# A decoder layer's head: loads in order of need, one square per bank summed from SBUF, x's squares spread, six slot numbers moved

## The chip, the cores and the metric

The kernel is one program on one core of a Trainium2 chip. The metric is the time of one execution on the device in microseconds (us). Before the change it is 2418.71 us, the median of three runs (2417.26 to 2421.04).

The core has five engines that run their own instruction streams: PE (TensorE, the matrix multiplies), DVE (VectorE), ACT (ScalarE), POOL (GpSimd) and SP (SyncE, which here issues most of the transfers). They meet at semaphores only. Data lie in DRAM, in SBUF (128 partitions) and, for what PE accumulates, in the eight banks of PSUM.

## What is computed

One hybrid decoder layer on 512 tokens of width 2048, in fp32:

```
h = rms_norm(x, g_mix);  z = h @ w_in      # columns: attn q,k,v | ret q,k,v | ret gate
a = moba_attention(rope(rms_norm(q)), rope(rms_norm(k)), v)     # 8 heads of 128
r = silu(gate) * rms_norm(retention(rope(q), rope(k), v)) * g_ret   # 8 heads of 128
x = x + concat(a, r) @ w_o
h2 = rms_norm(x, g_ffn);  x = x + (silu(h2 @ w_gate) * (h2 @ w_up)) @ w_down
x = x + (p @ w_ple_proj) * sigmoid(rms_norm(x, g_ple) @ w_ple_gate + b)
```

Two norms matter here. The row norm of x (its 16 blocks of 128 x 512 are squared and summed) is not applied to h; its factor `rstd[0]` is applied to what is made of h. Query and key are normed for each head of 128 columns; the squares for that norm are those that the change rewrites.

## The kernel before

**Products.** Every fp32 operand is split into a high part and the remainder: `split` lets ACT write the high part (`wh` of a weight, `h`'s high half) and DVE subtract it (`wl`, the low half). A product is three matmuls: high by high, high by low, low by high (`mm3`, L73 to L76). For a weight unit of 128 x 1024 (`raw`, 512 KB) that is one ACT and one DVE instruction; `wh` and `wl` have three buffers each.

**Stages.** (1) `Plain`: the query and key columns of head pair 0, eight weight units of 24 matmuls, which accumulate into four banks (Y0, Y1, Z0, Z1). Beside it the 16 chunks of x transposed are loaded, scaled by ACT (`h_chunk`, L445) and split into `h`. (2) Three `Group`s of `w_vg` (values, values, gates). A Group forms a 1024-column block by seven products, in the order 1, 5, 6, 3, 7, 2, 4, of four units and twelve matmuls each; between products DVE adds weight quarters (`plus` on `raw`, L82). Products 5, 6, 3 and 7 need sums of chunks of x too: `first_factors(k)`, k from 0 to 7, loads chunks 2k and 2k+1 once more, into two buffers each (tags `e1`, `e5`), and makes the factors `s` from them (DVE L79, ACT, DVE L55). (3) The "mix": four attention pairs and four retention pairs. While a pair's projection runs (32 slots of six matmuls, some 1.36 us each), the score and weight products of the pair before it are put between the slots by hand: `heads` gives slot numbers to `at_slot`. (4) `w_ow`, the gate/up, down and per-layer-embedding products, all as Groups.

**The head's callback.** `run` goes through the steps of stages 1 and 2, from i = -3; at step i it multiplies step i, splits step i+2 and adds for step i+3, and calls `beside(i)` first: chunks of x for `h` and Plain's weights (i from -2 to 5), `first_factors` (i from 5 to 12), first weights of the Groups (i from 3), and two of the sixteen `xn` loads with their squares at each step from 17 to 24.

**What sets the order.** A scheduler orders the instructions of each engine at build time, by its own model. Only what goes through `keep_in_program_order` stays as written: all of PE's work in the mix does; in the head before nothing does. Buffers tie steps together: `x`, `xn`, `zeros` and the copies `z0` share four buffers of tag `o`, and a load into one waits until its last reader is done. SP issues its loads in order: one that waits holds all behind it.

**Pair norms.** `evac` in `qk_attn` takes one bank: DVE multiplies by the two rotary tables (`z`, and `m` in two halves), ACT squares each head's 128 columns with a running sum (`squares`, L437: four ACTIVATEs and four reads of the accumulator), DVE adds `z` and `m`, and a `tensor_scalar` and a power on POOL make the norm factor `rs`, by which ACT scales the key columns (L670). The projection of the next pair writes the same four banks, so each bank is free once its last reader here is done. Pair 0's `z` comes from DRAM, stored at Plain's end; its squares were taken from the banks there (`ms0`).

Of the kernel before, what the change touches and what calls it, by code (L numbers as in the profile page):

```python
# [10 lines left out]
F32 = mybir.dt.float32  # L11
# [22 lines left out]
def layer_kernel(ctx, tc, x, xT, pT, g_mix, wqk, w_vg, qk_norm, g_ret, w_ow, g_ffn,  # L34
# [46 lines left out]
    def plus(o, a, b):  # L81
        nc.vector.tensor_tensor(o, a, b, op=ALU.add)  # L82
# [122 lines left out]
    class Group:  # L205
# [8 lines left out]
        def load(self, q, u):  # L214
            t = rawq.tile([P, 2, T], F32, name="raw", tag={"11": "l1", "12": "bd"}.get(q, "c"))
            nc.sync.dma_start(t, self.src(int(q[0]) - 1, int(q[1]) - 1, self.units[u]))
            self.raw[q, u] = t
# [178 lines left out]
    class Plain:  # L396
# [5 lines left out]
        def load(self, u):  # L402
            self.raw[u] = rawq.tile([P, 2, T], F32, name="raw", tag="l1" if u < 4 else "c")
            nc.sync.dma_start(self.raw[u], wqk[0, u])

# [3 lines left out]
        def extract(self, p, u):  # L409
            self.w[u] = [wq.tile([P, 2, T], F32R, name=n, tag=n) for n in ("wh", "wl")]  # L410
            split(*self.w[u], self.raw[u])

# [12 lines left out]
        def evac(self):  # L425
            for b in range(NB):
                t = ev_tile("o", 4, name="z0")
                nc.scalar.activation(t, self.acc[b], AF.Copy)
                nc.sync.dma_start(zd[b], t)
                squares(ms0[b], ev_tile("v", name="sq"), self.acc[b])  # L430

    zd = [dram.tile([P, T], F32, name=f"z_{b}") for b in range(NB)]
    ms0 = [stat.tile([P, 4], F32, name="ms0", bufs=NB) for _ in range(NB)]

    def squares(ms, junk, of):
        for j in range(4):
            nc.scalar.activation(junk[:, j * HD:(j + 1) * HD], of[:, j * HD:(j + 1) * HD],  # L437
                                 AF.Square, accum_out=ms[:, j:j + 1])

    first = Plain()  # L440

    def h_chunk(k, tag="o", bufs=4):
        t = ev_tile(tag, bufs, name="x")
        nc.sync.dma_start(t, xT[k * P:(k + 1) * P, :])
        nc.scalar.activation(t, t, AF.Copy, scale=gm[:, k:k + 1])  # L445
        return t
# [37 lines left out]
    groups[0].next, groups[1].next = groups[1:]  # L484
    nc.sync.dma_start(ident, ident_c)
    nc.sync.dma_start(gf, g_ffn)
    nc.sync.dma_start(gp, g_ple)
    nc.sync.dma_start(gr, g_ret)

    def beside(i):  # L490

        if -2 <= i < NC // 2 - 2:
            for k in (2 * i + 4, 2 * i + 5):
                t = h_chunk(k)
                split(h[:, k, 0, :], h[:, k, 1, :], t)
            first.load(i + 2)
        if 5 <= i < 5 + NC // 2:
            first_factors(i - 5)
        for at, q in ((3, "11"), (7, "12"), (11, "22")):
            if at <= i < at + 4:  # L500
                groups[0].load(q, i - at)
        if 17 <= i < 25:
            for u in range(2):
                b, s = divmod(2 * (i - 17) + u, NS)
                t = ev_tile("o", 4, name="xn")
                nc.sync.dma_start(t, x[b * P:(b + 1) * P, s * T:(s + 1) * T])
                nc.scalar.activation(t, t, AF.Square, accum_out=ssq[0][:, b, s:s + 1])
        elif i == 25:
            rstd_of(ssq[0], rstd[0])
# [135 lines left out]
    def qk_attn(i):  # L645

        made, norms = [], []

        def evac(b, acc, ms=None):
            z = rp_tile("z", (P, 2, 2, HD))  # L650
            m = rm_tile("m", (P, 2, 2, 2, HD // 2))
            a4 = acc.rearrange("p (s h d) -> p s h d", s=2, h=2)
            a5 = acc.rearrange("p (s h u e) -> p s h u e", s=2, h=2, u=2)
# [3 lines left out]
            for u in range(2):  # L657
                nc.vector.tensor_tensor(m[:, :, :, u], a5[:, :, :, 1 - u],
                                        sn[:, :, b, None, u * half:(u + 1) * half].to_broadcast([P, 2, 2, half]),
                                        op=ALU.mult)  # L660
            if ms is None:
                ms = stat.tile([P, 4], F32, name="ms")
                squares(ms, rm_tile("sq"), acc)
            plus(z, z, m.rearrange("p s h u e -> p s h (u e)"))
            nc.vector.tensor_scalar(ms, ms, 1.0 / HD, eps1[:, b:b + 1], op0=ALU.mult, op1=ALU.add)
            rs = stat.tile([P, 4], F32, name="rs", tag="rsqk", bufs=2 * NB)
            power(rs, ms, 4)
            z3 = z.rearrange("p s h d -> p (s h) d")
            for j in (2, 3):
# [4 lines left out]
        if i == 0:  # L674
            for b in range(NB):
                evac(b, z0[:, b].rearrange("p c e -> p (c e)").bitcast(F32), ms0[b])
        else:
            for b, acc in enumerate(projection(True)):
                evac(b, acc)
        return made, norms  # L680
# [160 lines left out]
    def heads(i, made):  # L841
# [5 lines left out]

        at_slot(17 if i <= NPAIR else 8, lambda: v.append(v_of(i)))
        if i < NPAIR:
# [7 lines left out]
            if i == 0:  # L857
                plan = [(n + 3, fn) for n, fn in plan]
        else:
            for j, (at, steps_s, steps_n, last) in enumerate(((8, (11, 12, 13, 14), (17, 18), 24),  # L860
# [6 lines left out]
            if i == NPAIR:  # L867
                plan = [(n + 6, fn) for n, fn in plan]
        for n, fn in plan:
# [211 lines left out]
```

## Time and profile before

| what | us |
|---|---|
| median of three runs | 2418.71 |
| the profiled execution, its own time | 2423.45 |
| its span | 2421.7 |
| PE busy | 2337.6 (97%) |
| DVE busy | 1938.8 (80%) |
| ACT busy | 1222.2 (50%) |

Times in the trace are counted from the start of the span. Matmuls of 512 columns follow each other at 0.227 us where PE was granted its full clock (2.4 GHz) and at 0.43 us at the half (1.2 GHz); a granted clock of 0.83 over a stretch means that part of it ran at the half. A line of a timeline gives the start, the busy time, the engine, the line in the kernel, the operation, the output and inputs with their shapes and the count; in square brackets how long the engine sat idle before it and whose signal ended that. A line of waits gives who waited for whom, the sum in us, the number of waits and the longest. `SPq` is SP's own issuing.

### The profile page before, as it was taken

What the parts mean: (1) busy time and instruction counts of PE and PEld (TensorE: products, weight loads), DVE (VectorE), ACT (ScalarE), POOL (GpSimd) and SP (SyncE); (2) the same over time, 40 slices, a digit from 0 to 9 for tenths busy, and PEclk for the clock granted to TensorE, in tenths of its full rate; (3) what the DMA queues carried; (4) which work ended last, traced back from release to release, by engine and by line L of the source; (5) the groups of instructions that cost most, each with busy time, mean ns of one, the idle gap of its engine ahead of it and who ended that gap; (6) DMA issues with size and microseconds to landing.
All of it is one profiled execution on the core that took longest, in us unless ns stands there. A gap on an engine that the chain in (4) does not pass through costs nothing.

```text
span 2421.7 us, 29331 instructions
## 1 busy us (share of the span) xinstructions
PE 2337.6 (97%) x10470; PEld 1910.3 (79%) x10470; DVE 1938.8 (80%) x2608; ACT 1222.2 (50%) x1918; POOL 43.4 (2%) x47
## 2 busy tenths in 40 slices
PE   8899999999998998999999999999999999999998
PEld 6688877777887876888888888888878878888777
DVE  5888766665668898789888988889878877789997
ACT  7754434444445555455544554455544433456643
POOL 0100000000001000000000000000000000000000
PEclk8999999999999999999999999999999999999999
DMA  8446543335657866454356444654595676767763
GB/s 297 141 172 209 157 149 115 118 124 153 181 167 255 317 204 257 140 182 141 121 160 196 148 133 132 188 174 139 171 393 175 245 284 208 294 239 243 275 208 122
DMA packets 168260, 467.81 MB, mean 193 GB/s; under 512 B 18737, under 2 KB 31409, under 8 KB 163121
## 3 DMA queue, kind: packets, MB, share of 16 engines
q1 hardware_dynamic: 164128, 457.53, 55.7%
q10 hardware_dynamic: 2704, 4.20, 0.7%
q0 software_dynamic: 1280, 4.20, 0.4%
q8 instruction: 82, 1.34, 0.2%
q14 instruction: 66, 0.53, 0.1%
HBM read 356.28 MB, written 105.38 MB: 191 GB/s over the span
## 4 chain that ended last, share of the span: by engine, by line
PE 74%; DVE 13%; DMA 7%; issue 3%; ACT 2%; POOL 0%; SPq 0%; ACTq 0%; DVEq 0%; POOLq 0%
PE Y L64 27%; PE Z L64 18%; PE X L64 16%; PE acc L64 8%; DVE wl L55 4%; DVE raw L82 3%; PE at L64 2%; DMA h<-o 2%; PE tp L69 2%; DMA x<-in_xT 1%; ACT wh L54 1%; DVE t L79 1%; DMA mr<-zr 1%; DVE o L55 1%; DVE s L55 1%
## 5 line engine op out<-in xcount | busy, mean ns | idle before, releaser
L54 ACT ACTIVATE wh<-raw 128x1024 fp32r<-128x1024 f32 x727 | 769.3, 1060 | 832.6 <-PE Y L64 293.9
L55 DVE TENSOR_TENSOR wl<-raw,wh 128x1024 fp32r<-128x1024 f32 x727 | 884.3, 1221 | 288.6 <-ACT wh L54 287.5
L64 PE MATMUL Y<-wh,s 128*128 128x512 f32 x2160 | 681.7, 391 | 12.7 <-ACT wh L54 12.7
L64 PEld LDWEIGHTS Y<-wh,s 128*128 128x128 f32 x2160 | 405.3, 188 | 101.1 <-ACT wh L54 18.3
L64 PE MATMUL Z<-wh,s 128*128 128x512 f32 x1504 | 478.0, 393 | 4.2 <-DMA s<-h 2.0
L82 DVE TENSOR_TENSOR raw<-raw 128x1024 f32<-128x1024 f32 x376 | 453.9, 1220 | 25.7 <-DMA raw<-in_w_gu 10.3
L64 PE MATMUL Y<-wl,s 128*128 128x512 f32 x1080 | 424.7, 393 | 1.4 <-DVE wl L55 1.2
L64 PE MATMUL X<-wh,s 128*128 128x512 f32 x1312 | 418.3, 394 | 8.0 <-ACT wh L54 5.2
L64 PEld LDWEIGHTS Z<-wh,s 128*128 128x128 f32 x1504 | 283.1, 189 | 64.0 <-DMA s<-h 2.3
L64 PE MATMUL Z<-wl,s 128*128 128x512 f32 x752 | 298.1, 397 | 4.7 <-DVE wl L55 4.7
L64 PEld LDWEIGHTS X<-wh,s 128*128 128x128 f32 x1312 | 248.4, 190 | 62.0 <-ACT wh L54 7.4
L64 PE MATMUL X<-wl,s 128*128 128x512 f32 x656 | 259.1, 395 | 4.7 <-DVE wl L55 4.5
L64 PEld LDWEIGHTS Y<-wl,s 128*128 128x128 f32 x1080 | 203.4, 188 | 45.4 <-DVE wl L55 4.1
L64 PEld LDWEIGHTS Z<-wl,s 128*128 128x128 f32 x752 | 142.3, 189 | 37.4 <-DVE wl L55 8.4
L64 PE MATMUL acc<-h,wh 128*128 128x512 f32 x512 | 162.4, 399 | 2.2 <-ACT sq L437 2.2
L64 PEld LDWEIGHTS X<-wl,s 128*128 128x128 f32 x656 | 124.2, 189 | 34.2 <-DVE wl L55 8.3
L64 PE MATMUL acc<-wh,h 128*128 128x512 f32 x384 | 133.6, 405 | 4.6 <-ACT sq L437 4.2
L64 PEld LDWEIGHTS acc<-h,wh 128*128 128x128 f32 x512 | 93.4, 191 | 19.7 <-ACT sq L437 3.5
L64 PE MATMUL acc<-h,wl 128*128 128x512 f32 x256 | 100.9, 394 | 0.0
L64 PEld LDWEIGHTS acc<-wh,h 128*128 128x128 f32 x384 | 73.5, 192 | 21.5 <-ACT sq L437 6.4
L64 PE MATMUL acc<-wl,h 128*128 128x512 f32 x192 | 76.1, 396 | 0.0
L79 DVE TENSOR_TENSOR e<-Y,e 128x512 f32<-128x512 f32 x96 | 62.9, 683 | 14.2 <-PE Y L64 14.2
(196 smaller groups left out, 2099.2 us busy)
## 6 DMA issues: line engine op xcount, KB each, us to landing
raw<-in_w_gu SPq DMA_DIRECT2D x176, 512.0 KB, 4.3
raw<-in_w_dn SPq DMA_DIRECT2D x88, 512.0 KB, 5.8
a<-o SPq DMA_DIRECT2D x154, 256.0 KB, 2.5
raw<-in_wqk SPq DMA_DIRECT2D x64, 512.0 KB, 3.7
s<-a SPq DMA_DIRECT2D x14, 2048.0 KB, 10.5
raw<-in_w_vg SPq DMA_DIRECT2D x48, 512.0 KB, 4.7
raw<-in_w_ow SPq DMA_DIRECT2D x32, 512.0 KB, 5.7
xin<-x SPq DMA_DIRECT2D x64, 256.0 KB, 5.8
```

Of the source, the lines that this page charges most:

```text
L54: nc.scalar.activation(H, src, AF.Copy)
L55: nc.vector.tensor_tensor(L, src, H.bitcast(F32), op=ALU.subtract)
L64: ins = nc.tensor.matmul(*args, **kw)
L69: ins = nc.tensor.transpose(o, a, ident)
L79: nc.vector.tensor_tensor(o, a, b, op=ALU.subtract)
L82: nc.vector.tensor_tensor(o, a, b, op=ALU.add)
```

## The change

1. **Order of the head's loads.** Loads of x, of Plain's weights, of the first Group's weights and of `xn` go through `keep_in_program_order`. The first weight unit is loaded in two halves of 256 KB ahead of the first chunk of x and split in halves; the loads of `ident`, `gf`, `gp` and `gr` are written at step 3.
2. **Plain's end.** The four banks are copied and stored only; the sixteen squares there and `ms0` are gone.
3. **x's squares.** One `xn` block a step, at steps 0 to 5 and 13 to 22, and the norm factor at step 24 (before: two a step at 17 to 24 and the factor at 25).
4. **Pair norms.** One ACT Square of 128 x 512 for each bank into an SBUF tile `sq` (tag `pt`, two buffers), and one DVE `tensor_reduce` over it instead of four squares with running sums; for pair 0 too. `evac` becomes `rotate` and `norm`, called as rotate(0), rotate(1), norm(0), norm(1), then the same for 2 and 3.
5. **Slots.** What attention pair 3 had planned at slots over 32 comes four slots later; retention pair 4's plan is 9 slots late instead of 6, and its value load is at slot 20 instead of 17.

```diff
@@ Plain @@
-            nc.sync.dma_start(self.raw[u], wqk[0, u])
+            if u == 0:
+                for c in range(2):
+                    tc.keep_in_program_order(nc.sync.dma_start(self.raw[u][:, c], wqk[0, u, :, c]))
+            else:
+                tc.keep_in_program_order(nc.sync.dma_start(self.raw[u], wqk[0, u]))
...
-            split(*self.w[u], self.raw[u])
+            if u:
+                return split(*self.w[u], self.raw[u])
+            for c in range(2):
+                split(*(w[:, c] for w in self.w[u]), self.raw[u][:, c])
...
-                squares(ms0[b], ev_tile("v", name="sq"), self.acc[b])
@@ beside @@
-            first.load(i + 2)
+            if i > -2:
+                first.load(i + 2)
...
-        if 17 <= i < 25:
-            for u in range(2):
-                b, s = divmod(2 * (i - 17) + u, NS)
...
+        done = i if 0 <= i < 6 else i - 7 if 13 <= i < 23 else None
+        if done is not None:
+            b, s = divmod(done, NS)
+            t = ev_tile("o", 4, name="xn")
+            tc.keep_in_program_order(nc.sync.dma_start(t, x[b * P:(b + 1) * P, s * T:(s + 1) * T]))
+            nc.scalar.activation(t, t, AF.Square, accum_out=ssq[0][:, b, s:s + 1])
@@ qk_attn @@
-        def evac(b, acc, ms=None):
+        def rotate(b, acc):
...
+            sq = ap.tile([P, T], F32, name="sq", tag="pt", bufs=2)
+            nc.scalar.activation(sq, acc, AF.Square)
...
-            if ms is None:
-                ms = stat.tile([P, 4], F32, name="ms")
-                squares(ms, rm_tile("sq"), acc)
-            plus(z, z, m.rearrange("p s h u e -> p s h (u e)"))
+            return z, m, sq
+
+        def norm(b, z, m, sq):
+            ms = stat.tile([P, 4], F32, name="ms")
+            nc.vector.tensor_reduce(ms, sq.rearrange("p (j d) -> p j d", j=4), axis=AX.X, op=ALU.add)
...
+            plus(z, z, m.rearrange("p s h u e -> p s h (u e)"))
...
+        for pair in ((0, 1), (2, 3)):
+            got = [rotate(b, accs[b]) for b in pair]
+            for b, g in zip(pair, got):
+                norm(b, *g)
@@ heads @@
-        at_slot(17 if i <= NPAIR else 8, lambda: v.append(v_of(i)))
+        at_slot(17 if i < NPAIR else 20 if i == NPAIR else 8, lambda: v.append(v_of(i)))
...
+            elif i == NPAIR - 1:
+                plan = [(n + 4 if n > 32 else n, fn) for n, fn in plan]
...
-                plan = [(n + 6, fn) for n, fn in plan]
+                plan = [(n + 9, fn) for n, fn in plan]
```

What the engines' instruction streams make of it, at three places. First SP's first loads; `x` is a chunk of x transposed, `raw` from `in_wqk` a weight unit of Plain. Before:

```order
L485 DMA ident<-in_ident_c 128x128
L486 DMA gf<-in_g_ffn 128x16
L487 DMA gp<-in_g_ple 128x16
L488 DMA gr<-in_g_ret 128x8
L444 DMA x<-in_xT 128x512 x2
L404 DMA raw<-in_wqk 128x1024
L444 DMA x<-in_xT 128x512
L404 DMA raw<-in_wqk 128x1024 x3
L444 DMA x<-in_xT 128x512
L404 DMA raw<-in_wqk 128x1024 x2
```

and after the change:

```order
L408 DMA raw<-in_wqk 128x512 x2
L445 DMA x<-in_xT 128x512 x3
L491 DMA ident<-in_ident_c 128x128
L491 DMA gf<-in_g_ffn 128x16
L491 DMA gp<-in_g_ple 128x16
L491 DMA gr<-in_g_ret 128x8
L445 DMA x<-in_xT 128x512
L410 DMA raw<-in_wqk 128x1024
L445 DMA x<-in_xT 128x512 x2
L410 DMA raw<-in_wqk 128x1024
L509 DMA xn<-in_x 128x512
L445 DMA x<-in_xT 128x512 x2
```

The weights no longer run ahead of x, the first weight stands first, and a third stream (`xn`) comes between.

Second DVE at the end of pair 1's projection, from the release of bank 0 to that of bank 3 (each bank: `z`, two `m`). Before, from bank 1's `z`:

```order
L655 TENSOR_TENSOR z<-acc,rope 128x512
L658 TENSOR_TENSOR m<-acc,rope 128x4x64 x2
L665 TENSOR_SCALAR ms<-ms,eps_2486 128x4
L55 TENSOR_TENSOR o<-o 128x256
L655 TENSOR_TENSOR z<-acc,rope 128x512
L82 TENSOR_TENSOR z<-z,m 128x512
L55 TENSOR_TENSOR PL<-tp,PH 128x128
L658 TENSOR_TENSOR m<-acc,rope 128x4x64 x2
L655 TENSOR_TENSOR z<-acc,rope 128x512
L665 TENSOR_SCALAR ms<-ms,eps_2486 128x4
L55 TENSOR_TENSOR wl<-raw,wh 128x1024
```

and after the change, from the same `z`:

```order
L661 TENSOR_TENSOR z<-acc,rope 128x512
L664 TENSOR_TENSOR m<-acc,rope 128x4x64 x2
L671 TENSOR_REDUCE ms<-sq 128x4
L55 TENSOR_TENSOR PL<-tp,PH 128x2x128
L661 TENSOR_TENSOR z<-acc,rope 128x512
L664 TENSOR_TENSOR m<-acc,rope 128x4x64 x2
L671 TENSOR_REDUCE ms<-sq 128x4
L82 TENSOR_TENSOR z<-z,m 128x512
L672 TENSOR_SCALAR ms<-ms,eps_2465 128x4
L661 TENSOR_TENSOR z<-acc,rope 128x512
L664 TENSOR_TENSOR m<-acc,rope 128x4x64 x2
```

A `TENSOR_REDUCE` comes to DVE for each bank; bank 3 is still the last to be read.

Third DVE where attention pair 3's last two score blocks (`at`, 384 and 512 columns) meet the rotary work (`zr`, `mr`, `qkL`) of retention pair 4. Before:

```order
L55 TENSOR_TENSOR wl<-raw,wh 128x1024
L701 TENSOR_TENSOR at<-at,sides 128x128
L752 TENSOR_TENSOR zr<-zr,mr 128x512
L701 TENSOR_TENSOR at<-at,sides 128x128
L55 TENSOR_TENSOR qkL<-zr,qkH 128x512
L703 TENSOR_REDUCE mx<-at 128x1 x2
L55 TENSOR_TENSOR qkL<-zr,qkH 128x512
L705 TENSOR_SCALAR mx<-mx,rs 128x1
L55 TENSOR_TENSOR wl<-raw,wh 128x1024
L705 TENSOR_SCALAR mx<-mx,rs 128x1
L709 RECIPROCAL sm<-sm 128x1
L710 TENSOR_SCALAR pt<-pt,sm 128x384
```

and after the change:

```order
L55 TENSOR_TENSOR wl<-raw,wh 128x1024
L762 TENSOR_TENSOR zr<-zr,mr 128x512
L55 TENSOR_TENSOR wl<-raw,wh 128x1024
L711 TENSOR_TENSOR at<-at,sides 128x128
L713 TENSOR_REDUCE mx<-at 128x1
L715 TENSOR_SCALAR mx<-mx,rs 128x1
L711 TENSOR_TENSOR at<-at,sides 128x128
L719 RECIPROCAL sm<-sm 128x1
L713 TENSOR_REDUCE mx<-at 128x1
L720 TENSOR_SCALAR pt<-pt,sm 128x384
L55 TENSOR_TENSOR qkL<-zr,qkH 128x512
```

The score blocks' work, which PE waits for, now stands after most of the rotary work in one run.

## Rows read from the trace of the kernel before

**Rows 1.** The page: busy time, share of the span and instructions of each engine.

```profile
PE 2337.6 (97%) x10470; PEld 1910.3 (79%) x10470; DVE 1938.8 (80%) x2608; ACT 1222.2 (50%) x1918; POOL 43.4 (2%) x47
```

**Rows 2.** PE's timeline at eight places, from the warm-up to the mix.

```profile
1.23 4.01 PE L394 MATMUL tp<-zeros 128*128 128x512 bf16 x10 [1.23 <-DVE zeros L389]
9.99 1.22 PE L64 MATMUL Y<-wh,h 128*128 128x512 f32 x2 [4.75 <-ACT wh L54]
...
36.21 0.79 PE L64 MATMUL Y<-wh,h 128*128 128x512 f32 x1 [4.57 <-ACT h L54]
...
95.94 0.73 PE L64 MATMUL Y<-wh,s 128*128 128x512 f32 x2 [3.60 <-ACT wh L54]
...
307.68 0.47 PE L64 MATMUL acc<-wh,h 128*128 128x512 f32 x1 [0.38 <-DVE e L79]
...
329.98 2.28 PE L69 MATMUL tp<-ident,z 128*128 128x128 f32 x4 [3.02 <-DVE z L82]
...
436.27 0.50 PE L64 MATMUL acc<-wh,h 128*128 128x512 f32 x1 [1.65 <-ACT sq L437]
...
568.67 0.88 PE L69 MATMUL tp<-ident,pt 128*128 128x128 f32 x3 [4.37 <-DVE pt L710]
```

**Rows 3.** Stretches: length; busy (count) PE, PEld, DVE, ACT, POOL; PE clock; DMA; GB/s.

```profile
8.00:15.00 7.00, 5.01 (x12) 4.00 (x13) 5.20 (x6) 5.20 (x8) 0.00 (x0) 0.51 1.01 402
35.30:42.20 6.90, 5.99 (x14) 4.74 (x15) 2.69 (x5) 6.08 (x11) 0.00 (x0) 0.51 1.04 392
...
64.00:100.00 36.00, 27.77 (x105) 20.67 (x104) 28.59 (x47) 31.96 (x95) 1.92 (x1) 0.91 0.57 175
...
560.00:580.00 20.00, 15.63 (x64) 12.76 (x64) 11.62 (x22) 6.09 (x11) 0.00 (x0) 0.83 0.31 97
```

**Rows 4.** SP's timeline of the first microseconds (issuing alone, not landing).

```profile
0.74 0.39 SPq L485 DMA_DIRECT2D ident<-in_ident_c  x1
...
2.60 0.91 SPq L444 DMA_DIRECT2D x<-in_xT  x2
3.55 0.43 SPq L404 DMA_DIRECT2D raw<-in_wqk  x1
```

**Rows 5.** ACT's timeline: the first chunk of x, the first weight.

```profile
5.39 0.72 ACT L445 ACTIVATE x<-x,gm 128x512 f32<-128x512 f32 x1 [2.60 <-DMA x<-in_xT]
...
8.88 1.06 ACT L54 ACTIVATE wh<-raw 128x1024 fp32r<-128x1024 f32 x1 [0.77 <-DMA raw<-in_wqk]
```

**Rows 6.** DMA of 20 to 45 us: totals; an issue line's count, size, median landing.

```profile
DMA packets 3883, 9.56 MB, mean 382 GB/s; under 512 B 430, under 2 KB 430, under 8 KB 3881
...
x<-in_xT SPq DMA_DIRECT2D x14, 256.0 KB, 6.5
```

**Rows 7.** DMA of 60 to 100 us.

```profile
xn<-in_x SPq DMA_DIRECT2D x16, 256.0 KB, 4.1
```

**Rows 8.** DVE's costliest forms of 10 to 100 us: count, busy, mean ns, idle before.

```profile
L55 DVE TENSOR_TENSOR wl<-raw,wh 128x1024 fp32r<-128x1024 f32 x19 | 23.1, 1222 | 12.1 <-ACT wh L54 12.1
L82 DVE TENSOR_TENSOR raw<-raw 128x1024 f32<-128x1024 f32 x12 | 14.6, 1221 | 0.1
L55 DVE TENSOR_TENSOR s<-t,s 128x256 fp32r<-128x256 f32 x28 | 10.7, 419 | 4.1 <-ACT s L54 3.9
```

**Rows 9.** DVE's timeline at the mix's start, pair 1's end, pair 3's end.

```profile
329.24 2.49 DVE L82 TENSOR_TENSOR z<-z,m 128x512 f32<-128x512 f32 x4
...
425.61 0.68 DVE L655 TENSOR_TENSOR z<-acc,rope 128x512 f32<-128x512 f32 x1
...
568.10 0.42 DVE L710 TENSOR_SCALAR pt<-pt,sm 128x384 f32<-128x384 f32 x1
```

**Rows 10.** DVE's forms of 300 to 570 us: the 512-column reduce.

```profile
L703 DVE TENSOR_REDUCE mx<-at 128x1 f32<-128x512 f32 x8 | 5.5, 684 | 0.1
```

**Rows 11.** POOL's timeline: a norm factor's power.

```profile
430.02 1.01 POOL L85 TENSOR_TENSOR rs<-ms,neghalf 128x4 f32<-128x4 f32 x1 [56.58 <-DVE ms L665]
```

**Rows 12.** PE's waits of 372 to 560 us: sum, number, longest.

```profile
PE acc L64 <- ACT sq L437: 6.4, 7, 1.7
```

More of the change, by code (lines that the diff above doesn't have):

```diff
@@ L215, in load @@
             t = rawq.tile([P, 2, T], F32, name="raw", tag={"11": "l1", "12": "bd"}.get(q, "c"))
-            nc.sync.dma_start(t, self.src(int(q[0]) - 1, int(q[1]) - 1, self.units[u]))
+            ins = nc.sync.dma_start(t, self.src(int(q[0]) - 1, int(q[1]) - 1, self.units[u]))
+            if self is groups[0]:
+                tc.keep_in_program_order(ins)
             self.raw[q, u] = t
@@ L429, in evac @@
                 nc.sync.dma_start(zd[b], t)
-                squares(ms0[b], ev_tile("v", name="sq"), self.acc[b])
     zd = [dram.tile([P, T], F32, name=f"z_{b}") for b in range(NB)]
[L433 to L438, printed above, removed]
     first = Plain()
@@ L443, in h_chunk @@
         t = ev_tile(tag, bufs, name="x")
-        nc.sync.dma_start(t, xT[k * P:(k + 1) * P, :])
+        ins = nc.sync.dma_start(t, xT[k * P:(k + 1) * P, :])
+        tc.keep_in_program_order(ins)
         nc.scalar.activation(t, t, AF.Copy, scale=gm[:, k:k + 1])
@@ L484, in layer_kernel @@
     groups[0].next, groups[1].next = groups[1:]
[L485 to L488, printed above, removed]
     def beside(i):
+        if i == 3:
+            for t, c in ((ident, ident_c), (gf, g_ffn), (gp, g_ple), (gr, g_ret)):
+                nc.sync.dma_start(t, c)
         if -2 <= i < NC // 2 - 2:
+            if i == -2:
+                first.load(0)
             for k in (2 * i + 4, 2 * i + 5):
@@ L501, in beside @@
                 groups[0].load(q, i - at)
-        if 17 <= i < 25:
-            for u in range(2):
-                b, s = divmod(2 * (i - 17) + u, NS)
[L505 to L508, printed above, removed]
+        done = i if 0 <= i < 6 else i - 7 if 13 <= i < 23 else None
[4 more added lines that the diff above has]
+            nc.scalar.activation(t, t, AF.Square, accum_out=ssq[0][:, b, s:s + 1])
+        elif i == 24:
             rstd_of(ssq[0], rstd[0])
@@ L674, in qk_attn @@
         if i == 0:
-            for b in range(NB):
-                evac(b, z0[:, b].rearrange("p c e -> p (c e)").bitcast(F32), ms0[b])
-        else:
-            for b, acc in enumerate(projection(True)):
-                evac(b, acc)
+            accs = [z0[:, b].rearrange("p c e -> p (c e)").bitcast(F32) for b in range(NB)]
+        else:
+            accs = projection(True)
+        for pair in ((0, 1), (2, 3)):
+            got = [rotate(b, accs[b]) for b in pair]
+            for b, g in zip(pair, got):
+                norm(b, *g)
         return made, norms
```

## The prediction

> **What bounds the kernel now.** I read the page first: PE is busy 97% of the span, DVE 80% [rows 1]. Nothing speeds the kernel up unless PE waits less or runs less at its half clock, so the next views were PE's timeline for its gaps [rows 2] and the stretches for its clock [rows 3]. PE idles 84 us of the span, and three places that the change touches show long gaps: the head (up to the mix), the ends of the attention pairs, and the end of attention pair 3.
>
> The head can be booked whole. Plain has 192 matmuls and three Groups have 3 x 7 x 4 x 12 = 1008; at 0.227 us each that is 272.4 us. PE's first real matmul is at 9.99 and the mix starts at 307.68 [rows 2], 297.7 us later, so 25.3 us are lost on the way. They are: the half clock at 8 to 15 us, where PE was busy 5.0 us at 0.51, half of it lost, 2.5; the gap of 4.57 before 36.21 and the half clock after it, busy 6.0 at 0.51, 3.0 lost [rows 2, 3]; in 64 to 100, 36.0 - 27.8 = 8.2 idle and a clock of 0.91, which is 6.5 us at the half and 3.2 lost, 11.4 together [rows 3]; and 3.8 scattered. The 9.99 itself: SP issues four small constants first, so the first chunk of x is issued at 2.60 and used at 5.39, and the first weight is issued at 3.55 and used at 8.88 [rows 4, 5]. In 20 to 45 us the transfers saturate at 382 GB/s, because weights for the Groups run ahead of x's chunks, which then land in 6.5 us instead of the 2.8 of the first one [rows 4 to 6]. That is the gap at 36.21.
>
> **First loads: -3.4 us, and -2.5 of half clock.** The halves are issued at 0.74 and about 1.2 (the places of the constants, [rows 4]) and, with the 2.8 us of the first chunk, land at 3.5 and 4.0; the two ACT splits of 128 x 512 (half of the 1.06 of [rows 5] each) end at 4.6. The first chunk of x is issued third, at 1.65, and lands at 4.5 to 5.0; ACT scales two chunks (0.72 each, [rows 5], less some overlap) and writes the first high half (0.53): PE starts at 6.3 to 7.3, I take 6.6 against 9.99. PE's warm-up matmuls end at 5.24 [rows 2], so it then idles 1.4 us instead of 4.75. The gap of 1.65 us before 436.27 did not take the clock (that matmul took 0.50, the one after the 4.57 gap 0.79), those of 4.4 and 4.6 did [rows 2, 3], so I expect the full clock from the start; if not, +2.5.
>
> A rule speaks against the halving: the Trainium skill, "DMA: Bandwidth & Descriptors", section "Bandwidth", wants transfers of at least 1 MiB, and its section "Anatomy of one DMA" fits about 2.0 us fixed for each one, measured for transfers issued by GpSimd. If the two halves paid that one after the other, the first product would come 2.0 us later, and the forecast would be 2399. No row shows two halves of one weight.
>
> **Plain: -7.6 us, 0 to 5 given back.** With loads strictly by need the 4.57 gap and its 3.0 us of half clock go: Plain would end at 6.6 + 43.6 = 50.2 instead of about 64. What is next late is the ring of four `o` buffers, which `xn` now shares: the second chunk of a step can be issued only when the first chunk of the step before has been split, and ACT does that after both its scalings. A round is the issue's 0.4 [rows 4], the landing, a scaling, a high and a low half (0.6 each) and a signal or two, about landing + 2.3 us, against 5.46 us of PE's work a step. With landings of 2.8 to 4.1 [rows 4, 5 and 7] that is 5.1 to 6.4, so PE loses between nothing and some 5 us over Plain. Demand at PE's pace is 1.25 to 1.8 MB in 5.46 us, 229 to 330 GB/s, under the 382 of [rows 6]; I take the landing of `xn`'s rows and no net loss, as the last chunk is wanted only at 44.8.
>
> **Group 1's opening: DVE becomes the bound.** Until the factor of product 5 for the last chunks (`first_factors(7)`) is there, DVE must do 17 `wl` and 12 adds (start to start 1.13, the 1.22 of [rows 8] less 0.09 of overlap), some 60 short ones of 256 columns (0.34, from 0.42 in [rows 8]) and 16 splits of h (0.6): 32.8 + 20.4 + 9.6 = 62.8 us. It begins near 7, but Plain's three weight buffers pace it, and the last four factors' loads stand in SP's queue behind the stores of the four banks, which wait for Plain's end near 52. Counting DVE's new row through gives that factor at 84. PE's work up to there is Plain 43.5, product 1 10.9, product 5 but its last half unit 9.5, and 4.5 of product 6 that stands before it: 68.4, so PE comes at 75 and waits 9 us in several pieces. I add 1.0 for half clock (0 if each piece is short, 3.4 as after 95.94 otherwise). The squares of Plain's end and ten of the sixteen `xn` squares leave ACT here, which by this count isn't the late one any more. So the mix starts at 6.6 + 272.4 + 10 + 3.8 = 292.8 instead of 307.7. **Head: -15**, between -7 (A below) and -22 (no wait at the opening).
>
> **Mix start: +3 (0 to +6).** Here PE waits 3.02 us for pair 0's first turned `z`, behind DVE's four additions [rows 2, 9]. Their squares were ready before; now ACT squares from SBUF, DVE has four reduces (0.68 each, 0.6 start to start, [rows 10]) and POOL the power (1.0, [rows 11]) in the same chain. The key columns' scaling on ACT waits for that; two to three reduces, a short `tensor_scalar` and the power on the path make 3.1 us.
>
> **Pair ends: -2 (-4 to +1).** PE waits seven times for the last reader of a bank, 6.4 us in all, 1.65 of it for bank 3 of pair 1 [rows 2, 12]. ACT's four squares and four reads a bank become one square, and it no longer ends last; but DVE gets a reduce for each bank. From bank 0's `z` at 425.61 [rows 9] to PE's 436.27 are 10.7 us; DVE's new row is, in starts, `z` 0.6 and `m` 0.66 four times, three reduces 1.8, two additions 1.2, a `wl` 1.13 and small ones 0.6 up to bank 3's last `m`: 9.8. So 0.8 at each of three ends, less a little. Had DVE one more `wl` to do in it, the gain is gone.
>
> **Pair 3's end: -7.4 (-7.8 to 0).** PE waits 4.37 us for the scaled scores `pt`, since DVE does retention pair 4's rotary work first (`pt`'s scaling starts at 568.10), and then runs at the half clock: the stretch's 0.83 is 6.8 us at the half, 3.4 lost [rows 2, 3, 9]. Four slots are 5.4 us: the transposes come due at 569.4. In the new row the score blocks stand behind the rotary work and get DVE at once: a reduce of 0.68 at most [rows 10], a scaling of 0.42 [rows 9], and with the mask and the exponential some 3 us, an estimate from these; from matmuls due at 564.3, `pt` at 567.3. Both parts go, but 0.4 for the 512-column block. Behind it retention pair 4's plan is three slots later; what that may cost is C below.
>
> **Sum.** -15 + 3.1 - 2 - 7.4 = -21.3, and the rest 0 (the scheduler moves DVE's and ACT's rows in the retention too, of either sign, 5 us). The profiled execution is 2423.45; less 21.3 is 2402.2. The median of the runs is 4.7 under the profiled one, so **2397 us**.
>
> **Rivals.**
> A, the opening takes back the head: DVE's 62.8 us do not shrink, and if it is idle more in Plain than I counted, the mix starts only 5 us earlier. For it: DVE idles 12.1 us before its `wl` in 10 to 100 already [rows 8]. Against: the factors' first four are done during Plain. 2407 us.
> B, the buffer ring is the bound, and the kernel gets slower: if the chunks land in about 10 us, half as long again as the median of [rows 6], a round is 12.5 us, Plain ends near 83, and with PE waiting 7 us a step it loses its clock each time, some 8 us more; the opening's 9 us then go. Mix at 324, +16, with the other terms +10: 2428 us. It turns to slower at landings over some 9.5 us. Against: the 6.5 of [rows 6] came with weights far ahead of x in the same queue.
> C, the slots bring nothing, because the wait moves to retention pair 4's own later scores or to the value load that comes three slots later: 2404 us.
> That the loads would not come earlier at all is not possible with the order kept.
>
> **How the numbers follow.** The forecast has 0.50, A 0.20, C 0.17, B 0.07, and 0.06 remains for an opening without waits (2390). A measurement of this kernel can tell about 0.2%, 4.8 us. Faster than 2413.9 are the forecast, A, C and the last but for the tail that the retention's 5 us and the mix start's 6 make: 0.83; within, 0.10; slower, B, 0.07. The range runs from the head's -22 with the forecast's other terms, and a little of the rest, 2386, to A with the mix start at its dear end, 2412.
>
> **What would show it.** PE's first `h` matmul near 6.6 at the full clock; no gap in Plain; waits for DVE and no clock loss over 3.4 us between 69 and 87; the mix at 293. At its start a gap near 6 us that ends with POOL or ACT's scaling. At pair ends DVE's `m` or the reduce, not ACT's square, as the releaser. At pair 3's end no gap over 1 us. It is wrong if chunks of x land in over 5 us, if the mix starts after 303, or if the retention's waits grow by more than 5 us.

## The result and the profile after

The changed kernel takes 2432.34 us (median of four runs, 2430.99 to 2436.52) where the kernel before took 2418.22 beside it: a ratio of 1.0059, 95% interval 1.0042 to 1.0077. It is slower by 0.6%, outside the range of the prediction and on the other side. The profiled execution took 2431.26 us, its span is 2429.5.

PE's busy time fell by 6 us, its share too, so it waits 14 us more. Page of after, first line of the engines (answers [rows 1]):

```profile
PE 2331.4 (96%) x10470; PEld 1903.0 (78%) x10470; DVE 1947.9 (80%) x2625; ACT 1217.1 (50%) x1807; POOL 37.7 (2%) x47
```

Both kernels issue the same number of matmuls, in nearly the same order, so the start of the n-th matmul can be compared. This table is worked out from the records of the traces; a negative number means that PE is ahead of the kernel before (profiled executions; e1 and e9 are experiments below):

```
n-th matmul, place                before    after     e1      e9     (after, e1, e9 less before)
   11  Plain's first                10.6     -2.5    -2.7    -2.0
 1200  end of the third Group      304.9     -8.8    -7.8    -8.2
 1350  after the mix's start       344.6     -5.5    -5.1    -6.8
 1500  after pair 1's end          377.0     -2.3    -1.9    -6.8
 2250  before pair 3's end         541.6     -1.0    -1.8    -6.1
 2400  after pair 3's end          580.6     -6.9    -7.7   -12.0
 2700  in retention pair 4's heads 642.7     -3.8    -4.7   -13.3
 3150  end of the mix              736.6     -5.6    -2.6   -13.2
 3300  first product of w_ow       772.0     +9.5    -3.0   -13.3
 3450                              804.8    +12.3    -3.0   -13.3
 4050  end of w_ow                 948.5     +6.9    -4.3   -12.8
 7950                             1826.5     +4.3    -4.2   -12.4
 9800  before the last Groups     2250.1     +5.0    -3.9   -11.2
10200  near the end               2350.2     +7.9    -0.0    -7.4
```

Up to the end of the mix the change had gained 5.6 us. Then 18 us are lost at one place, where no edit of the change seemed to be. PE's timeline of after at seven places (start, busy, engine, line, operation, shapes, count, idle before and its releaser); the first, second and fourth answer 9.99, 329.98 and 568.67 of [rows 2], the third is pair 1's end, the fifth is in retention pair 4:

```profile
7.71 0.50 PE L64 MATMUL Y<-wh,h 128*128 128x512 f32 x1 [2.03 <-ACT h L54]
...
322.89 1.08 PE L69 MATMUL tp<-ident,z 128*128 128x128 f32 x2 [4.74 <-DVE z L82]
...
365.14 0.47 PE L64 MATMUL acc<-wh,h 128*128 128x512 f32 x1 [2.11 <-DVE m L664]
...
570.96 0.63 PE L69 MATMUL tp<-ident,pt 128*128 128x128 f32 x4 [0.47 <-DVE pt L720]
...
620.53 1.26 PE L69 MATMUL tp<-ident,r 128*128 128x128 f32 x4 [3.62 <-DVE r L821]
...
765.40 0.79 PE L64 MATMUL X<-wh,s 128*128 128x512 f32 x1 [17.21 <-ACT wh L54]
...
2292.37 0.73 PE L64 MATMUL Y<-wh,s 128*128 128x512 f32 x2 [1.89 <-ACT wh L54]
```

The 17.21 us is followed back through two engines. ACT's timeline of after: its split of the first `w_ow` weight waited for a transfer.

```profile
764.29 1.06 ACT L54 ACTIVATE wh<-raw 128x1024 fp32r<-128x1024 f32 x1 [13.11 <-DMA raw<-in_w_ow]
```

SP's timeline of after shows when that transfer was issued, and behind what:

```profile
743.59 1.39 SPq L837 DMA_DIRECT2D s<-mix  x3
...
751.20 0.32 SPq L837 DMA_DIRECT2D s<-mix  x1
751.57 16.87 SPq L216 DMA_DIRECT2D raw<-in_w_ow  x12
```

and the same engine before:

```profile
667.09 0.34 SPq L216 DMA_DIRECT2D raw<-in_w_ow  x1
```

Before, the twelve loads go out one or two at a time from 667 us on, as buffers come free; after, all twelve come in one run at 751.6, behind the last reload of the mix's factors (`s<-mix`, paced by copies at the mix's end), the first of them 84 us later. The stretch from 740 to 790 us (length; busy PE, PEld, DVE, ACT, POOL; clock; DMA; GB/s), first after, then before:

```profile
740.00:790.00 50.00, 29.72 (x144) 24.71 (x143) 27.09 (x40) 18.62 (x42) 4.85 (x8) 0.80 0.81 310
```

```profile
740.00:790.00 50.00, 46.97 (x232) 39.33 (x233) 40.22 (x62) 26.73 (x57) 7.83 (x11) 1.00 0.66 245
```

PE is 17 us less busy, and the clock of 0.80 means that the half was granted for some 20 of the 50 us, most of which PE idled.

The code has the reason. `Group.load` pins its transfer if `self is groups[0]`. The name `groups` is bound anew further down, for the list that begins with the first Group of `w_ow`; the function looks the name up when it is called, so that Group's loads are pinned too, behind what was written on SP just before them: the paced reloads.

### The profile page after: what moved, and what is told of

It reads as the page before. It is cut to its first block, busy times and chain, and to the rows that moved or that the text cites. A ratio compares the mean times of both kernels' runs of the same rounds, so it can differ in the third digit from the quotient of the medians.

```text
span 2429.5 us, 29213 instructions
## 1 busy us (share of the span) xinstructions
PE 2331.4 (96%) x10470; PEld 1903.0 (78%) x10470; DVE 1947.9 (80%) x2625; ACT 1217.1 (50%) x1807; POOL 37.7 (2%) x47
## 4 chain that ended last, share of the span: by engine, by line
PE 74%; DVE 12%; DMA 7%; issue 3%; ACT 3%; SPq 1%; POOL 0%; ACTq 0%; DVEq 0%; POOLq 0%
PE Y L64 27%; PE Z L64 18%; PE X L64 17%; PE acc L64 9%; DVE wl L55 4%; DVE raw L82 3%; PE at L64 2%; PE tp L69 2%; ACT wh L54 1%; DMA raw<-in_w_pl 1%; DMA h<-o 1%; DMA pp<-pp 1%; DMA raw<-in_w_ow 1%; DVE t L79 1%; DMA x<-in_xT 1%
## 5 line engine op out<-in xcount | busy, mean ns | idle before, releaser
L54 ACT ACTIVATE wh<-raw 128x1024 fp32r<-128x1024 f32 (+1 forms) x728 | 768.6, 1058 | 823.4 <-PE Y L64 292.1
L55 DVE TENSOR_TENSOR wl<-raw,wh 128x1024 fp32r<-128x1024 f32 (+1 forms) x728 | 883.0, 1218 | 275.3 <-ACT wh L54 274.5
L64 PEld LDWEIGHTS X<-wl,s 128*128 128x128 f32 x656 | 124.1, 189 | 36.4 <-DVE wl L55 10.7
```

The costliest lines, as they stand in the source:

```text
L54: nc.scalar.activation(H, src, AF.Copy)
L55: nc.vector.tensor_tensor(L, src, H.bitcast(F32), op=ALU.subtract)
L64: ins = nc.tensor.matmul(*args, **kw)
```

## The experiments

Each ran beside the kernel before on the same chip, ten to twelve timed runs for most. Ratios are to the kernel before, with the 95% interval. A profiled execution differs from the median of its kernel's runs by up to 5 us either way, so gaps are read from traces and verdicts from ratios.

**e1: the pin for the head alone.**

```diff
+    lead = []
...
-            if self is groups[0]:
+            if self in lead:
...
+    lead.append(groups[0])
```

(`lead` gets the first Group of the first list only.)

> The changed kernel, with only the first Group of the head pinned in program order; the loads of w_ow are left to the scheduler again, and stand early in SP's stream as before. Theory (the test 'self is groups[0]' is true a second time, for the first Group of w_ow, since the name groups is bound anew, and pins its twelve loads behind the paced reloads of the mix's factors): the 17.2 us gap at 748 is gone, with the half clock behind it, 15 to 18 us less than the changed kernel, 2414 to 2418 us; PE's place at the first w_ow product some 5 to 6 us ahead of the kernel before instead of 9.5 behind. Rival (the later slots of pair 3 and retention pair 4 push the stores and so the w_ow loads): the gap stays, 2430 to 2434.

2422.49 us, ratio 1.0012 (1.0003 to 1.0021). The loads go out early again (SP's timeline of e1):

```profile
662.41 0.35 SPq L217 DMA_DIRECT2D raw<-in_w_ow  x1
```

and the 17 us gap is gone: in the table e1 has no step at 3300. But the gain is 0.47%, 11 us, not 15 to 18: with the gap, after had lost less than before at two later places (the table's steps to 4050 and 7950, 5.4 and 2.6 us; in 930 to 950 us its clock was 1.00 where before has 0.74), and without it those losses are there again. So the pin explains 0.47 of the 0.59%; freed of it, the change is still no gain.

**e2: the kernel before with nothing but that pin.**

```diff
+            if self in lead:
+                tc.keep_in_program_order(ins)
...
+    lead.append(groups[0])
```

(Here `lead` gets the first Group of `w_ow`.)

> The kernel before, with nothing but the twelve first loads of w_ow pinned behind what was written on SP ahead of them. Theory: the first of these loads is issued some 85 us later, a gap of 15 to 18 us opens at the first w_ow product, 2433 to 2437 us. Rival (the pin alone does nothing, it is the slots or the longer norm chain): 2416 to 2420.

2437.55 us, ratio 1.0078 (1.0064 to 1.0091): 19 us. The same wait, alone (SP's timeline and PE's waits of 700 to 800 us in e2):

```profile
751.05 17.22 SPq L217 DMA_DIRECT2D raw<-in_w_ow  x12
```

```profile
PE X L64 <- ACT wh L54: 17.3, 1, 17.3
```

That settles the cause of the 17 us gap, which makes the change slower: the slots and the norms have no part in it. What follows asks where the forecast's 21 us went besides.

**e3: e1 with the old pair norms** (four squares with running sums a bank, no reduce; pair 0's too, from SBUF).

```diff
-            nc.scalar.activation(sq, acc, AF.Square)
...
-            nc.vector.tensor_reduce(ms, sq.rearrange("p (j d) -> p j d", j=4), axis=AX.X, op=ALU.add)
...
+                squares(ms, rm_tile("sq"), acc)
...
+            for b, acc in enumerate(projection(True)):
+                evac(b, acc)
```

> As e1, with the pair norms of the kernel before (four squares with running sums on ACT for each bank, no reduce on DVE; pair 0's squares are taken from SBUF at the mix's start, as in the change). Theory (the reduces on DVE stand ahead of the next bank's products and hold the banks longer): PE's waits at the three pair ends fall from about 10 to about 6.5 us, 4 us less than e1 (1 to 8 less). Rival (the pair ends are late for the later transposes and weights, not for the reduces): within 1 us of e1.

2417.96 us, ratio 0.9993 (0.9984 to 1.0001), 4.6 us under e1. PE's waits of 340 to 372 us, pair 1's end, in e1 and then in e3:

```profile
PE acc L64 <- DVE m L666: 4.3, 4, 2.1
```

```profile
PE acc L64 <- ACT sq L652: 1.5, 1, 1.5
```

So the norms cost here what they were to save. But the time that the reduces take is not the reason. DVE's timeline of after at that end, with bank 0's `z`:

```profile
356.14 0.23 DVE L727 TENSOR_SCALAR PL<-ident 128x128 fp32r<-128x128 f32 x1 [0.55 <-PE at L64]
...
357.35 0.43 DVE L55 TENSOR_TENSOR o<-o 128x256 fp32r<-128x256 f32 x1 [0.84 <-ACT o L54]
359.43 0.29 DVE L55 TENSOR_TENSOR PL<-tp,PH 128x128 fp32r<-128x128 f32 x1 [1.66 <-ACT PH L54]
359.92 0.69 DVE L661 TENSOR_TENSOR z<-acc,rope 128x512 f32<-128x512 f32 x1 [0.20 <-ACT sq L657]
```

and before:

```profile
359.41 1.22 DVE L55 TENSOR_TENSOR wl<-raw,wh 128x1024 fp32r<-128x1024 f32 x1
360.54 0.68 DVE L655 TENSOR_TENSOR z<-acc,rope 128x512 f32<-128x512 f32 x1
```

PE is 5.5 us ahead here (the table at 1350), so a `z` at the same place in PE's work would start at 355.1. It starts 4.9 later, and its row names who released it: ACT's square of the same bank. ACT's timeline of after:

```profile
359.12 0.28 ACT L54 ACTIVATE PH<-tp 128x128 fp32r<-128x128 f32 x1 [1.81 <-PE tp L69]
359.30 0.59 ACT L657 ACTIVATE sq<-acc 128x512 f32<-128x512 f32 x1
```

The change writes the square ahead of `z` (in `rotate`), the old code writes the squares behind `z` and `m`. In the trace of after each of the twelve `z` at the pair ends waits on ACT's semaphore and starts after its bank's square has ended (0.03 us after it for this one); before, `z` waits on PE's, and a bank's first square starts after its second `m`. So the order in which the two readers of a bank are written has turned round, and bank 0's square was put behind pair 0's first turned block (`PH`) in ACT's row. DVE's row has `z` late too, behind that block's low half, for which DVE idles 0.84 and 1.66 us; but with that wait an earlier place there would not have helped. From the start of bank 0's `z` to the end of bank 3's last `m` DVE then takes 9.8 us, against 9.6 in e3 without the reduces. This is read from the rows; a kernel with the reduces and the square behind `z` wasn't tried.

**e4: e1 with the old slots.**

```diff
-        at_slot(17 if i < NPAIR else 20 if i == NPAIR else 8, lambda: v.append(v_of(i)))
+        at_slot(17 if i <= NPAIR else 8, lambda: v.append(v_of(i)))
...
-            elif i == NPAIR - 1:
-                plan = [(n + 4 if n > 32 else n, fn) for n, fn in plan]
...
-                plan = [(n + 9, fn) for n, fn in plan]
+                plan = [(n + 6, fn) for n, fn in plan]
```

> As e1, with the slot numbers of the kernel before. Theory from the two traces: the 4.4 us gap at attention pair 3's last scores and its half clock come back (+5.9 us by the n-th matmul's start), the 3.6 us gap in retention pair 4 goes (-3.1): 3 us more than e1 (0 to 6). Rival (the slots bring nothing): the same as e1 within 1 us.

2419.17 us, ratio 0.9999 (0.9990 to 1.0008), 3 us under e1, though the intervals overlap: the other way than both had it. PE's waits of 555 to 640 us in e4 have the old one at pair 3's end:

```profile
PE tp L69 <- DVE pt L722: 4.1, 1, 4.1
```

so the slots do what the table shows at 2400, and lose it again behind. Step by step against e1, e4 is 4.2 us worse there (2250 to 2400), 3.9 better in retention pair 4 (2400 to 2700), 1.1 better before it (1500 to 2250) and 2.6 better in the last stage (9900 to 10200; see e12).

**e6: e1 with retention pair 4's second head's norm and last transposes three slots later still.**

```diff
-                plan = [(n + 9, fn) for n, fn in plan]
+                plan = [(n + (9 if n < 25 else 12), fn) for n, fn in plan]
```

> As e1_pin_head_only, but retention pair 4's second head gets its norm and its last transposes three slots later still (its scores stay). Theory (its norm at slots 34 and 35 falls on DVE's rotary work for retention pair 5, which ends some 2 us after the norm is due): the 3.6 us gap at its transposes falls under 1.5 us and the half clock after it goes, 3 us under e1. Rival (the chain from its products to the norm is too long wherever it stands, or the wait moves to pair 5's first scores): within 1 us of e1.

2418.52 us, ratio 0.9990 (0.9982 to 0.9999), 5 us under e1. The wait before that head's transposes, PE's waits of 600 to 640 us in e1 and 600 to 650 in e6:

```profile
PE tp L69 <- DVE r L823: 3.7, 1, 3.7
```

```profile
PE tp L69 <- DVE r L823: 1.0, 1, 1.0
```

DVE's timeline of after shows the collision: the norm (`ms`) stands behind rotary work of the next pair and a weight's low half.

```profile
616.73 0.68 DVE L762 TENSOR_TENSOR zr<-zr,mr 128x512 f32<-128x512 f32 x1
617.33 1.22 DVE L55 TENSOR_TENSOR wl<-raw,wh 128x1024 fp32r<-128x1024 f32 x1
618.47 0.16 DVE L817 TENSOR_SCALAR ms<-ms 128x4 f32<-128x4 f32 x1
...
620.12 1.14 DVE L821 SCALAR_TENSOR_TENSOR r<-r,rs,sg 128x128 f32<-128x128 f32 x4 [0.90 <-POOL rs L85]
```

It is the collision that the slots removed at pair 3's end, one projection later: retention pair 4's plan, three slots later, ran into retention pair 5's rotary work.

**e5: the head alone** (e1 with the diffs of e3 and e4 together).

> As e1_pin_head_only, with the old pair norms and the old slot numbers: of the change only the head is left (loads by need with the first weight in halves, x's squares spread, Plain's end without squares). Theory (the parts add): e1 less 4.5 for the norms and 3.3 for the slots, as measured, about 2415, 4 to 5 us under the kernel before: the head's 9 us at the mix's start less what later stages give back. Rival (the head's gain is taken back before the end whatever stands behind it): within 1.5 us of the kernel before.

2419.21 us, ratio 0.9994 (0.9985 to 1.0003): the runs show 1.4 us, 3.6 at most, as the rival had it. But its trace does not show the gain taken back: PE is 8.6 us ahead at the mix's start, 9.1 at the 9800th matmul and 7.0 at the last one. The two profiled executions are far apart in their kernels' spread: e5's took 2416.40, 2.8 under its median, that of the kernel before 2423.45, 3.4 over the median of the runs beside e5. So some 6 of the 7 us lie between executions and not between kernels, and no trace shows in which stage.

**e7: e1 with x's squares at their old steps.**

```diff
-        done = i if 0 <= i < 6 else i - 7 if 13 <= i < 23 else None
-        if done is not None:
-            b, s = divmod(done, NS)
...
+        if 17 <= i < 25:
+            for u in range(2):
+                b, s = divmod(2 * (i - 17) + u, NS)
```

> As e1_pin_head_only, with x's squares where they were (two a step at steps 17 to 24, not pinned). Theory (the opening of the first Group is bound by DVE, and xn costs ACT and the queue little there): the mix starts within 1.5 us of e1, the same time within 1 us. Rival (xn in Plain takes buffers and ACT's time, so that its end comes late): the mix starts 2 to 5 us earlier. Other rival (xn at its old steps delays the last factors' loads): 3 to 6 us later.

2426.80 us, ratio 1.0024 (1.0015 to 1.0034), 3 us over e1. The end of the third Group is at the same place (296.98 us against 297.03), so the head doesn't feel it; the loss comes at the mix's start (2.1 us) and later, and what makes it isn't shown. By the medians spreading x's squares was worth it, but not where the prediction looked; the two intervals overlap.

**e8: e1 with the first weight whole.**

```diff
-            if u == 0:
-                for c in range(2):
-                    tc.keep_in_program_order(nc.sync.dma_start(self.raw[u][:, c], wqk[0, u, :, c]))
...
+            tc.keep_in_program_order(nc.sync.dma_start(self.raw[u], wqk[0, u]))
...
-            for c in range(2):
-                split(*(w[:, c] for w in self.w[u]), self.raw[u][:, c])
+            split(*self.w[u], self.raw[u])
```

> As e1_pin_head_only, with the first weight unit loaded and split whole, still ahead of x. Theory: PE's first product waits for the first chunk of x, not for the weight: the whole unit lands near 4.3 us and its high part is ready near 5.4, the first chunk of x then is scaled some 0.4 us later, so PE starts within 0.6 us of e1's 7.7, and the time is the same within 1 us. Rival (the halves hide 1 us or more of the weight's landing): PE starts 1.5 us later or more, and may start at the half clock, which adds 2.5 us.

2422.62 us, ratio 1.0011 (1.0002 to 1.0020), as e1. PE's first product is at 7.31 us against 7.55 in e1: the halves bring nothing, since the first chunk of x, not the weight, comes last. Nor do they land later: ACT, waiting for the transfer, starts on the second half at 4.47 in e1 and on the whole unit at 4.46 in e8.

**e10: e1 with pair 0's squares from the banks at Plain's end again.**

```diff
+                squares(ms0[b], ev_tile("v", name="sq"), self.acc[b])
...
-            ms = stat.tile([P, 4], F32, name="ms")
...
+            ms = stat.tile([P, 4], F32, name="ms") if i else sq
```

(In pair 0, `sq` is then `ms0[b]`, and its square and reduce are left out.)

> As e1_pin_head_only, but pair 0's sixteen squares are taken from the banks at Plain's end again, so that no square, reduce or norm of pair 0 stands at the mix's start. Theory: PE's wait for pair 0's first turned z falls from 4.7 us to about 3, and the second one (1.3) goes, 2.5 to 3.5 us under e1 there; the opening of the first Group, bound by DVE, loses at most 1 us by ACT's squares: 1.5 to 3.5 us under e1 in all. Rival (the squares on ACT delay the opening's high halves as much): within 1 us of e1.

2425.32 us, ratio 1.0017 (1.0007 to 1.0027), 1.2 us over e1: about the size of the rival. PE's waits of 300 to 345 us (the mix's start), e1 and then e10:

```profile
PE tp L69 <- DVE z L82: 5.9, 2, 4.6
```

```profile
PE tp L69 <- DVE z L82: 3.3, 4, 2.4
```

2.6 us of wait go there, and one comes in the head (PE's waits of 50 to 110 us in e10), where the rival had named the high halves: product 5 needs bank Z, which the squares hold.

```profile
PE Z L64 <- ACT sq L447: 4.5, 1, 4.5
```

The third Group ends 3.8 us later. Taking the squares away from Plain's end was worth 3.8 us, moving them to the mix's start cost 3.5.

**b2: the kernel before again**, one execution.

> The kernel before once more, for a second profiled execution: the first took 2423.5 us where the median of its runs is 2418 to 2420. If the head's loss differs from one execution to the next (gaps near the length at which the clock falls), the mix starts some 3 to 5 us earlier here than 307.7, and the head's gain by the first profile (8.9 us) was overstated by that. If not, the mix starts within 0.7 us of 307.7 and the 5 us lie in later stages.

2422.97 us. At the 1200th matmul it is 1.8 us ahead of the first profile, at the 9800th level with it. Against this execution the head's gain is 1.8 us smaller. But this one too is long for its kernel, whose medians in the five sets of runs lie between 2418.2 and 2422.2, so where a short execution gains stays open.

**e9: e1 with the old norms and e6's slots**, the diffs of e3 and e6 together.

> e1_pin_head_only with the old pair norms and e6's slots together. Theory (norms and slots stand in different places of the mix and add): e1 less 4.5 and less 4, 2413 to 2416, under both kernels. Rival (as the head's gain in e5, it is taken back behind the mix): 2417 to 2420.

2413.34 us, ratio 0.9970 (0.9960 to 0.9980). This beats both kernels: the head as changed, the pin kept to the head, the norms as before, and slots that collide at neither of the two places.

**e12: the kernel before with e9's slots alone.** To the kernel before:

```diff
-                plan = [(n + 6, fn) for n, fn in plan]
+                plan = [(n + (9 if n < 25 else 12), fn) for n, fn in plan]
```

and the two other lines of e4's diff the other way round.

> The kernel before with nothing but the slot numbers of e9: attention pair 3's last blocks four slots later, retention pair 4's plan nine, its second head's norm and transposes twelve. Theory (the slots bring what the traces show at pair 3's end, and the head's 6 to 9 us at the mix's start reach the end only in part): pair 3's 4.4 us gap and half clock go, 5 to 7 us under the kernel before, 2412 to 2415 where that has 2419, ratio 0.997 to 0.998. Rival (e9's gain needs the head): within 2 us of the kernel before.

2420.28 us, ratio 0.9995 (0.9986 to 1.0005): the rival. Its trace has the 5.9 us at pair 3's end and gives back 4.7 between the 9900th and the 10200th matmul. Others lose there too: after 3.2, e1 2.4, e5 3.0, e9 3.2, and e2, which has nothing but the pin, 5.1; the kernel before loses nothing there in either profile, nor does e4. The last stage's source is the same in all. ACT's timeline there, before and after:

```profile
2285.73 2.00 ACT L54 ACTIVATE wh<-raw 128x1024 fp32r<-128x1024 f32 x2 [1.05 <-DVE raw L82]
2287.64 0.58 ACT L294 ACTIVATE e<-Z 128x512 f32<-128x512 f32 x1
```

```profile
2290.29 1.08 ACT L296 ACTIVATE e<-Z 128x512 f32<-128x512 f32 x2 [0.97 <-PE Z L64]
2291.26 2.95 ACT L54 ACTIVATE wh<-raw 128x1024 fp32r<-128x1024 f32 x3
```

Before, the scheduler put two weights ahead of the copies of bank Z; after, both copies come first, and PE waits 1.89 us for the weight (the row at 2292.37) where it waited 0.17. In all fourteen traces the two go together: the two profiles of before and e4 have the first order and lose at most 0.2 us there, the eleven others have the second and lose 2.3 to 5.1. By these losses the order takes 0.12% from the head alone (e5), 0.19 from the slots alone (e12), and 0.13 from both together (e9) only once, which fits 0.9994, 0.9995 and 0.9970. No run moved that order by itself.

## Why the prediction was wrong

**The sum's "the rest 0", with 5 us for what the scheduler moves, is the step that failed.** SP's new row was read at the head, and behind the mix only as rows of DVE and ACT that move "in the retention". SP's row there has all twelve `w_ow` loads behind the paced reloads, and the diff has the line that does it; both could be read there before the forecast. e2 puts 19 us on it alone, e1 11 us in the changed kernel. The rivals did not have it either: the slower one, B, was another mechanism, and it did not occur: the transfers of 5 to 45 us in after (out, in, queue, count, KB each, median us from issue to landing):

```profile
x<-in_xT SPq DMA_DIRECT2D x18, 256.0 KB, 4.3
```

The chunks of x landed in 4.3 us where 6.5 was read before [rows 6] and B wanted over 9.5; Plain ran without one gap, and the mix started 8.8 us early, not 16 late.

The pin is not the only step: without it e1, 2422, still lies above the range. By the table the sum's own terms come to -8.8 + 3.4 + 4.5 - 5.9 + 3.1 = -3.7 instead of -21.3, the last 3.1 being what comes back in retention pair 4. Term by term:

**First loads.** Predicted 6.6 at the full clock, found 7.71 at the full clock: the two chunks of x landed 0.9 us apart, and each scaling waited. The gap of 2.03 did not take the clock, as said; that was luck, since in five of the ten profiled executions with this head or one near it (e5 to e9) it fell after that gap, here 1.80 to 2.78 us long, for some 3.4 us, 1.7 lost. The halves cost and bring nothing (e8: 7.31 with the weight whole, 7.55 with halves). The rule that the prediction weighed, the Trainium skill, "DMA: Bandwidth & Descriptors", sections "Bandwidth" and "Anatomy of one DMA", would have made the halves 2.0 us later; the 4.47 and 4.46 of e1 and e8 don't bear that out for loads that SP issues.

**The opening.** DVE as the bound held: seven waits for DVE or a weight split between 56 and 92 us, as in the 2.10 us one at 90.0. By the table the mix starts 8.8 us early where 15 was forecast. 1.1 of the difference is the first product. The rest is the opening: from 7.71 to the mix's start 18.7 us are lost where 13.8 were counted (10 and 3.8). The waits, 9.9, were right at 9; the half clock, 1.0 in the sum, was mis-sized at 3.2, and the scattered rest is 5.6 instead of 3.8. (The 3.4 that the prediction gives "after 95.94" is the time at the half there, which loses 1.7.) The stretch that answers one of [rows 3] shows the same 0.91 as before, 6.5 us at the half, 3.2 lost:

```profile
64.00:100.00 36.00, 28.07 (x100) 19.42 (x99) 32.77 (x52) 26.14 (x56) 0.00 (x0) 0.91 0.52 175
```

The squares at Plain's end were written off as not late; e10 shows that they held bank Z for 4.5 us.

**The mix's start.** +3.1 forecast, +3.4 found (table, 1200 to 1350). That pair 0's squares and reduces cost there is right, and e10 confirms it; the size is luck in part. The sign that was named, POOL or ACT's scaling as releaser, did not come: the two gaps, 4.74 and 1.26, end with DVE's additions. Ahead of the first of these DVE's new row has three reduces (1.9 us with a short one), and ahead of the third a weight's low half (1.1) that stood behind all four before and was not in the sum; POOL's power, 1.0 in the sum, is not on that path.

**Pair ends.** -2 forecast, +4.5 found (1350 to 2250), 3.2 of it at the first. The step that failed is the start of the count: 9.8 us from bank 0's `z` was right, but that this `z` now waits for ACT's square, and where that square stands in ACT's row, was not looked at. The old 10.7 us (425.61 to 436.27), which the prediction and [rows 9] call pair 1's, are pair 2's; pair 1's end takes 11.6 before (360.54 to 372.14).

**Pair 3's end.** -7.4 forecast, -5.9 found; the stretch of [rows 3] now has the full clock:

```profile
560.00:580.00 20.00, 19.53 (x94) 16.14 (x93) 13.14 (x26) 8.29 (x14) 0.00 (x0) 1.00 0.49 148
```

Rival C was half right: 3.1 us came back in retention pair 4 (2400 to 2700), at the place that e6 mends.

Without the pin and with these sizes, the last stage's 2 to 5 us taken off, no gain is left, as in e1 (2422). The head's 8.8 us at the mix's start are 7.0 at the end of e5's trace and 1.4 in the runs; the last stage took 3, and the rest lies between the profiled executions and stays open.

## What to carry to other kernels

When a scheduler orders the streams, a change has to be read over the whole of each queue's new row, and first on the queue that issues the loads: a load that moves behind a paced or waiting transfer costs its whole lead, wherever the edit was. A pin by a name or a list that is used again later reaches further than the lines around it. A block of work that is shifted to avoid a collision has to be followed until the next place where the engine that it avoided is busy: here it met the same rotary work one pair on. Where two engines read one bank, the order in which the program writes the two reads decided here who waits for whom.

## What the runs showed of the hardware

PE's timeline of after, in the opening, and of e8, at its first products:

```profile
78.03 1.22 PE L64 MATMUL Y<-wh,s 128*128 128x512 f32 x2 [1.61 <-ACT wh L54]
```

```profile
7.31 0.50 PE L64 MATMUL Y<-wh,h 128*128 128x512 f32 x1 [1.80 <-ACT h L54]
...
8.98 0.63 PE L64 MATMUL Z<-wh,h 128*128 128x512 f32 x1
9.41 0.63 PE L64 MATMUL Z<-wl,h 128*128 128x512 f32 x1
```

In after the gap of 1.61 us before 78.0, with one of 0.70 before 75.7, was followed by matmuls at the half clock, 0.43 us apart up to about 84.5. In e8 the gap of 1.80 was followed by the half clock from about 8.6 to 12 us. Yet gaps of 2.03 (at 7.7), 2.10 (at 90.0) and 2.11 us (at 365) in after cost nothing, nor did the 1.88 at e1's first product. So the length of the last gap alone does not tell whether the clock falls, not even at the same place; the sum in the prediction went by that length.
